# Splitting layer 1's mixer weights ahead, during layer 0's feed-forward, in a two-layer diffusion trunk on one core

## The chip, the core and the metric

The kernel runs on one NeuronCore of a Trainium2 chip. Its engines work side by side, each through its own queue of instructions in order: TensorE (PE, matrix products into PSUM), VectorE (DVE), ScalarE (ACT), GpSimd (POOL), and SyncE (SP), which here only issues transfers. GpSimd can issue transfers too. The metric is the device time of one execution in microseconds (us).

## The reference, cut to what matters

Two layers work on 512 latent tokens and 256 context tokens of width 1024, in float32. Layer 0 is attention beside a RWKV-7 recurrence, layer 1 a bidirectional RG-LRU block; each layer ends in a squared-ReLU feed-forward of width 4096.

```python
def trunk_layer(x, xc, c, c_ctx, mixer_fn, ...):
    mod_l = jnp.split(jax.nn.silu(c) @ mod_w + mod_b, N_MOD, axis=-1)
    ...
    y_l, y_c = mixer_fn(modulate(x, sh1, sc1), modulate(xc, csh1, csc1), *mixer_params, ctx_out=ctx_out)
    x = layer_norm(DEEPNORM_ALPHA * x + g1 * y_l, ln1_g, ln1_b)
    x = layer_norm(DEEPNORM_ALPHA * x + g2 * squared_relu_mlp(modulate(x, sh2, sc2), mlp_w1, mlp_w2), ln2_g, ln2_b)

def odd_mixer(hl, hc, w_in, conv_w, conv_b, ga_w, ga_b, gx_w, gx_b, lam, w_out, ctx_out):
    gate_l, xr_l = jnp.split(hl @ w_in, 2, axis=-1)
    ...
    xr_l = depthwise_conv(xr_l, conv_w, conv_b)
    ...
    y_lat = (jax.nn.gelu(gate_l) * (hs_l[0] + hs_l[1])) @ w_out
```

The matrix in question is layer 1's `w_in`, 1024 by 2048: columns 0 to 1023 make the gate, 1024 to 2047 the recurrence's input.

## The kernel before

**Products.** A float32 matrix is split in two parts that TensorE takes at its faster rate: `hi`, a copy rounded by a cast, and `lo`, the rest. A product is three matmuls per 128 rows of depth (`mm3`, lines 183 to 185): hi by hi, lo by hi, hi by lo. Weights come in tiles of 128 columns, `[128, 8, 128]`, 512 KB. `w_raw` (line 152) loads one on SyncE's queue into a buffer `wraw` (two of them), and `w_split` casts it to `whi` on ScalarE (line 130) and subtracts to `wlo` on VectorE (line 136); of `whi` and `wlo` there are three buffers each. A tile's buffers come free when its products are done. Products land in one of three PSUM banks `mm`, which come free when VectorE or ScalarE has read them.

**The feed-forward** (`mlp`) goes through the hidden width in four chunks. In each, eight tiles of the first matrix give products for two halves of the 768 tokens, 384 each; ScalarE takes the ReLU from PSUM (`mr`, line 425), VectorE squares it (`msq`, line 427), and the two split it to `uhi` and `ulo`. Then eight tiles of the second matrix give products that VectorE adds to `t` (line 450). In the last chunk the second matrix is gone through once for each half of the tokens, and each half is followed by its layer norm (`ln_half`): `lnrs` on GpSimd (line 347), `xn` on ScalarE, `hhi` and `t` on VectorE, some of `hlo` on GpSimd (line 396). The norm's output is the mixer's input.

**Fillers.** `fill`, called once per weight tile, runs the next entry of a list of side jobs. In layer 0's feed-forward these are 40 steps for the first sixteen blocks of layer 1's modulation. They load a tile of the modulation's weights into a buffer `mraw` (two of them), and `paced` queues each step's VectorE work behind the last product. When the first half's layer norm starts, all entries that are left run at once. Sixteen more modulation blocks (`mods_spare`, lines 247 to 257) follow the feed-forward: load to `mraw`, eight matmuls into `md`, a transpose.

**Layer 1's mixer** (`layer1_mixer`) goes through eight blocks of 128 channels. For each it takes one tile for the recurrence's input (`xt`) and one for the gate (`gt`) through `w_tiles`, evacuates (`xp`, line 576), convolves (`cy`, lines 589 and 591), casts and subtracts (`cyh`, `cyl`), makes four small products with the gate weights (`gwr`, line 581, split to `gwh`, `gwl`), takes tanh, exponential and square root (`ga`, `gx`, `tv`, line 624) and scans (line 643).

**Order.** A scheduler puts the instructions of each engine in order when the kernel is built, by its own times; the program's order decides where these are equal. `issue_after(x)` keeps an instruction behind x. Waits between engines are semaphores.

## Time and profile before

| | |
|---|---|
| median of 3 runs | 2084.34 us |
| these runs | 2079.3, 2084.34, 2087.86 us |
| profiled execution, own time | 2087.57 us |
| its span, first to last instruction | 2085.8 us |
| TensorE busy | 1932.2 us, 93% |
| VectorE busy | 1257.9 us, 60% |
| ScalarE busy | 852.5 us, 41% |
| GpSimd busy | 283.9 us, 14% |

Shares over the whole span are means over unlike stages. Times in the trace count from the span's start: layer 0's feed-forward lies from about 860 to 1436 us, its second layer norm ends near 1460, layer 1's mixer follows until about 1620. Chunk 2's second product lies from 1225 to 1293, chunk 3's first from 1293 to 1360, its second from 1360 to 1436.

### The profile page before, as it was taken

The page shows a single profiled execution, that of the slowest core. Times are in us where ns is not written, and L with a number is a line of the kernel's source. Part 1 is how long each engine was busy: PE and PEld are TensorE (multiplying, and loading weights), DVE is VectorE, ACT ScalarE, POOL GpSimd, SP SyncE. Part 2 cuts the span into 40 slices and gives each one's busy share as a digit, 9 for nine tenths or more (in the row PEclk, how much of TensorE's full clock was granted, in tenths as well). Part 3 has the DMA queues.
Part 4 walks back from the last instruction along what each step waited for, and adds up shares of the span by engine and source line. Part 5 has one row for each costly group of instructions (what it writes and reads, how often), then busy time and mean ns, then how long its engine had stood idle before and what let it go on. Part 6 is the DMA issues. An engine that isn't in the chain of part 4 may idle for free.

```text
span 2085.8 us, 39869 instructions
## 1 busy us (share of the span) xinstructions
PE 1932.2 (93%) x16130; PEld 1730.5 (83%) x16130; DVE 1257.9 (60%) x2583; ACT 852.5 (41%) x1479; POOL 283.9 (14%) x458
## 2 busy tenths in 40 slices
PE   7989888588999988999999999999989889999997
PEld 5767767466777767999999999998777779999997
DVE  4568766746666678774654333447699575444456
ACT  2555432524455443441231221334699444233242
POOL 0001222634435431100000000001000010000000
PEclk9999989889999998999999999999999999999999
DMA  9465544643423228332232222245521673333334
GB/s 348 140 190 179 146 132 117 171 115 93 125 65 91 67 67 253 101 87 84 83 103 81 61 61 61 66 126 157 151 72 56 199 196 102 98 96 94 99 102 142
DMA packets 411512, 249.21 MB, mean 119 GB/s; under 512 B 61200, under 2 KB 396096, under 8 KB 411200
## 3 DMA queue, kind: packets, MB, share of 16 engines
q1 hardware_dynamic: 408296, 243.58, 39.4%
q0 software_dynamic: 2848, 3.03, 0.7%
q8 instruction: 127, 2.08, 0.4%
q14 instruction: 57, 0.47, 0.1%
q10 hardware_dynamic: 184, 0.06, 0.0%
HBM read 209.38 MB, written 36.44 MB: 118 GB/s over the span
## 4 chain that ended last, share of the span: by engine, by line
PE 73%; DVE 10%; DMA 7%; ACT 5%; issue 2%; SPq 2%; POOL 0%; DVEq 0%; ACTq 0%; POOLq 0%
PE mm L183 18%; PE mm L184 18%; PE mm L185 18%; PE tr L183 2%; PE tr L184 1%; PE tr L185 1%; PE mm L883 1%; DVE wlo L136 1%; PE g L1393 1%; PE mm L874 1%; ACT whi L130 1%; DMA wraw<-in_l_mlp_w_dram 1%; DVE pr L1010 1%; PE g L1370 1%; DMA st<-rw_pq 1%
## 5 line engine op out<-in xcount | busy, mean ns | idle before, releaser
L183 PE MATMUL mm<-hhi,whi 128*128 128x384 f32 (+2 forms) x1504 | 491.8, 327 | 9.4 <-ACT f_k L719 6.1
L184 PE MATMUL mm<-hlo,whi 128*128 128x384 f32 (+2 forms) x1504 | 489.2, 325 | 0.6 <-DVE hlo L396 0.3
L185 PE MATMUL mm<-hhi,wlo 128*128 128x384 f32 (+2 forms) x1504 | 489.1, 325 | 0.0
L130 ACT CAST whi<-wraw 128x1024 fp32r<-128x1024 f32 x216 | 226.3, 1049 | 533.6 <-PE mm L184 444.8
L183 PE MATMUL mm<-uhi,whi 128*128 128x384 f32 (+1 forms) x1280 | 399.1, 312 | 4.6 <-DVE t L450 3.7
L185 PE MATMUL mm<-uhi,wlo 128*128 128x384 f32 (+1 forms) x1280 | 397.3, 311 | 3.6 <-DVE wlo L136 3.6
L184 PE MATMUL mm<-ulo,whi 128*128 128x384 f32 (+1 forms) x1280 | 396.7, 310 | 0.7 <-DVE ulo L136 0.7
L136 DVE TENSOR_TENSOR wlo<-wraw,whi 128x1024 fp32r<-128x1024 f32 x216 | 264.0, 1223 | 189.4 <-ACT whi L130 189.0
L183 PEld LDWEIGHTS mm<-hhi,whi 128*128 128x128 f32 x1504 | 287.8, 191 | 23.4 <-ACT f_k L719 6.3
L184 PEld LDWEIGHTS mm<-hlo,whi 128*128 128x128 f32 x1504 | 288.1, 192 | 11.6 <-DVE hlo L396 0.6
L185 PEld LDWEIGHTS mm<-hhi,wlo 128*128 128x128 f32 x1504 | 287.8, 191 | 11.4 <-issue 0.6
L183 PEld LDWEIGHTS mm<-uhi,whi 128*128 128x128 f32 x1280 | 243.0, 190 | 6.5 <-DVE t L450 4.0
L185 PEld LDWEIGHTS mm<-uhi,wlo 128*128 128x128 f32 x1280 | 243.1, 190 | 5.7 <-DVE wlo L136 4.9
L184 PEld LDWEIGHTS mm<-ulo,whi 128*128 128x128 f32 x1280 | 243.2, 190 | 1.3 <-DVE ulo L136 1.3
L450 DVE SCALAR_TENSOR_TENSOR t<-mm,g,t 128x256 f32<-128x256 f32 (+2 forms) x200 | 92.9, 481 | 226.9 <-PE mm L185 224.4
L347 POOL TENSOR_TENSOR lnrs<-lnrs,mhalf 128x1 f32<-128x1 f32 x20 | 10.7, 545 | 1007.6 <-DVE lnrs L346 1007.6
L1415 POOL TENSOR_SCALAR ds<-rv,rw_dd 64x64 f32<-64x64 f32 x176 | 85.7, 487 | 155.2 <-DVE rv L1429 144.6
L425 ACT ACTIVATE mr<-mm 128x384 f32<-128x384 f32 (+1 forms) x128 | 55.6, 434 | 83.5 <-PE mm L185 83.4
L130 ACT CAST uhi<-msq 128x384 fp32r<-128x384 f32 (+1 forms) x128 | 58.6, 458 | 75.8 <-DVE msq L427 75.8
L427 DVE SCALAR_TENSOR_TENSOR msq<-mm,mr 128x384 f32<-128x384 f32 (+1 forms) x128 | 62.3, 487 | 45.1 <-ACT mr L425 44.8
L136 DVE TENSOR_TENSOR ulo<-msq,uhi 128x384 fp32r<-128x384 f32 (+1 forms) x128 | 63.0, 492 | 33.2 <-ACT uhi L130 29.5
L1429 DVE SCALAR_TENSOR_TENSOR rv<-z,rw_dd,ds 64x64 f32<-64x64 f32 x176 | 49.7, 282 | 30.6 <-PE z L1427 25.8
(427 smaller groups left out, 2937.8 us busy)
## 6 DMA issues: line engine op xcount, KB each, us to landing
wraw<-in_l_mlp_w_dram SPq DMA_DIRECT2D x148, 512.0 KB
mraw<-in_l_mod_w_dram SPq DMA_DIRECT2D x48, 512.0 KB
wraw<-in_l_w_in_dram SPq DMA_DIRECT2D x36, 512.0 KB
wraw<-in_l_w_out_dram SPq DMA_DIRECT2D x32, 512.0 KB
mw<-in_l_mod_w_dram SPq DMA_DIRECT2D x16, 512.0 KB
wraw<-in_l_mod_w_dram SPq DMA_DIRECT2D x16, 512.0 KB
rw_pq<-pqbk SPq DMA_DIRECT2D x8, 768.0 KB
rw_bk<-pqbk SPq DMA_DIRECT2D x8, 768.0 KB
```

The costliest lines, as they stand in the source:

```text
L130: nc.scalar.copy(hi, src)
L136: e.tensor_tensor(out=lo, in0=src, in1=hi.bitcast(F32), op=ALU.subtract)
L183: nc.tensor.matmul(out, sh, mh, start=f, stop=False)
L184: nc.tensor.matmul(out, sh, ml, start=False, stop=False)
L185: ins = nc.tensor.matmul(out, sl, mh, start=False, stop=l)
L425: nc.scalar.activation(r, ps, AF.Relu)
L427: nc.vector.scalar_tensor_tensor(out=sq, in0=ps, scalar=0.0, in1=r, op0=ALU.max, op1=ALU.mult)
L450: nc.vector.scalar_tensor_tensor(out=t[:, m, x:y], in0=ps[:, x - a:y - a], scalar=g[:, m, s:s + 1], in1=t[:, m, x:y], op0=ALU.mult, op1=AL ...
L874: nc.tensor.transpose(ps[:, j * 128:(j + 1) * 128], p[:, (j0 + j) * 128:(j0 + j + 1) * 128], self.ident)
L883: nc.tensor.matmul(po[64 * e:64 * e + 64, :256], va[:, k0 // 128 + j, h * 64:(h + 1) * 64], pts[e][:, j, :], start=(j == 0), stop=(j == n ...
L1415: P.tensor_scalar(out=ds[d][H[e]], in0=rv[H[e], i, e, :], scalar1=dn[H[e]], scalar2=None, op0=ALU.mult)
L1429: V.scalar_tensor_tensor(out=rn[H[e], e, :], in0=zu[d][H[e], 1], scalar=dn[H[e]], in1=ds[d][H[e]], op0=ALU.mult, op1=ALU.add)
```

## The change

`presplit` makes a list of sixteen pieces, one for each 128 columns of `l1_w_in`. A piece loads its raw tile on GpSimd's queue into one `mraw` buffer, casts it on ScalarE into the other (`issue_after` the last `mr`), subtracts on VectorE in place (`issue_after` the last `msq`), and stores both to memory (`w_pre`) on GpSimd's queue. The pieces are appended to the fillers of layer 0's feed-forward, behind the 40 modulation steps, each followed by an empty entry. In the mixer `w_pre` loads the two split halves on SyncE's queue straight into `whi` and `wlo`; its casts and subtractions of `w_in`, and their `wraw` loads, are gone.

```diff
+    def presplit(self, ap, n):
+        nc = self.nc
+        self.pre = self.dram.tile([n, 2, 128, 8, 128], F32, name="w_pre")
+        for j in range(n):
+            raw, hi = (self.wp.tile([128, 8, 128], F32, tag="mraw", name=self.nm("mraw"), bufs=2) for _ in range(2))
+            lo = raw.bitcast(F32R)
+            nc.gpsimd.dma_start(raw, ap[:, 128 * j:128 * j + 128].rearrange("(k p) c -> p k c", p=128))
+            with self.tc.issue_after(self.paces[0].ins):
+                nc.scalar.copy(hi.bitcast(F32R), raw)
+            with self.tc.issue_after(self.paces[1].ins):
+                nc.vector.tensor_tensor(out=lo, in0=raw, in1=hi, op=ALU.subtract)
+            for i, x in enumerate((hi, raw)):
+                nc.gpsimd.dma_start(self.pre[j, i], x)
+            yield
+
+    def w_pre(self, js):
+        for i, j in enumerate(js):
+            w = [self.wp.tile([128, 8, 128], F32R, tag=t, name=self.nm(t), bufs=self.wbufs[1]) for t in ("whi", "wlo")]
+            for u, x in enumerate(w):
+                self.nc.sync.dma_start(x.bitcast(F32), self.pre[j, u])
+            yield i, w
...
-                    nc.scalar.activation(r, ps, AF.Relu)
+                    self.paces = [nc.scalar.activation(r, ps, AF.Relu)]
...
-                    nc.vector.scalar_tensor_tensor(out=sq, in0=ps, scalar=0.0, in1=r, op0=ALU.max, op1=ALU.mult)
+                    self.paces.append(nc.vector.scalar_tensor_tensor(out=sq, in0=ps, scalar=0.0, in1=r, op0=ALU.max, op1=ALU.mult))
...
-            xt, gt = self.w_tiles(w_in[:, D:2 * D], eng=XS), self.w_tiles(w_in[:, 0:D], eng=GS)
+            xt, gt = self.w_pre(range(8, 16)), self.w_pre(range(8))
...
                 self.fillers += [lambda b=b: run(self.mods_spare(1, [b])) for b in range(MODV, 16)]
+                ahead = self.presplit(I["l1_w_in"], 16)
+                self.fillers += [lambda: next(ahead), lambda: None] * 16
```

Three places of the built order. The first is VectorE at the start of chunk 2's second product; `t` is an evacuation (its product's number behind `mm`), `wlo` the split of a later tile. Before:

```order
L450 SCALAR_TENSOR_TENSOR t_9086<-mm_12885,g_0_9065,t_9086 128x384
L450 SCALAR_TENSOR_TENSOR t_9086<-mm_12911,g_0_9065,t_9086 128x128
L450 SCALAR_TENSOR_TENSOR t_9086<-mm_12911,g_0_9065,t_9086 128x256
L136 TENSOR_TENSOR wlo_13059<-wraw_13056,whi_13058 128x1024
L450 SCALAR_TENSOR_TENSOR t_9086<-mm_12944,g_0_9065,t_9086 128x384
```

Now:

```order
L475 SCALAR_TENSOR_TENSOR t_9086<-mm_12893,g_0_9065,t_9086 128x384
L475 SCALAR_TENSOR_TENSOR t_9086<-mm_12919,g_0_9065,t_9086 128x128
L475 SCALAR_TENSOR_TENSOR t_9086<-mm_12919,g_0_9065,t_9086 128x256
L136 TENSOR_TENSOR wlo_13081<-wraw_13078,whi_13080 128x1024
L186 TENSOR_TENSOR mraw_13071<-mraw_13071,mraw_13072 128x1024
L475 SCALAR_TENSOR_TENSOR t_9086<-mm_12959,g_0_9065,t_9086 128x384
L475 SCALAR_TENSOR_TENSOR t_9086<-mm_12985,g_0_9065,t_9086 128x128
L475 SCALAR_TENSOR_TENSOR t_9086<-mm_12985,g_0_9065,t_9086 128x256
L136 TENSOR_TENSOR wlo_13140<-wraw_13137,whi_13139 128x1024
L186 TENSOR_TENSOR mraw_13196<-mraw_13196,mraw_13197 128x1024
```

A piece's subtraction (`mraw`, line 186 now) stands between the split of a later tile and the next evacuation, here and for the two tiles that follow: four pieces in a row. Six more stand in the last product and its first layer norm.

The second place is GpSimd at the first half's layer norm. Before, its queue held only the norm's work there:

```order
L347 TENSOR_TENSOR lnrs_14174<-lnrs_14174,mhalf 128x1 [waits DVE_49,Pool_49]
L347 TENSOR_TENSOR lnrs_14195<-lnrs_14195,mhalf 128x1 [waits DVE_49,Pool_49]
L347 TENSOR_TENSOR lnrs_14216<-lnrs_14216,mhalf 128x1 [waits DVE_49,Pool_49]
L396 TENSOR_TENSOR hlo_9118<-hf_14235,hhi_9117 128x384 [waits DVE_49,PE_49]
```

Now (a wait on DMASW is one for a transfer of GpSimd's own queue):

```order
L188 DMA w_pre<-mraw_14206 128x1024 [waits DMASW6_49,DVE_49]
L182 DMA mraw_14245<-in_l_w_in_dram 128x8x128 [waits DMASW5_49,DMASW3_49]
L372 TENSOR_TENSOR lnrs_14287<-lnrs_14287,mhalf 128x1 [waits DVE_49,Pool_49]
L372 TENSOR_TENSOR lnrs_14308<-lnrs_14308,mhalf 128x1 [waits DVE_49,Pool_49]
L188 DMA w_pre<-mraw_14246 128x1024 [waits Activation_49]
L188 DMA w_pre<-mraw_14245 128x1024 [waits DMASW1_49,DVE_49]
L372 TENSOR_TENSOR lnrs_14329<-lnrs_14329,mhalf 128x1 [waits DVE_49,Pool_49]
L182 DMA mraw_14252<-in_l_w_in_dram 128x8x128 [waits DMASW6_49,DMASW0_49]
L421 TENSOR_TENSOR hlo_9118<-hf_14348,hhi_9117 128x384 [waits DVE_49,PE_49]
```

The loads and stores of pieces 13 and 14 stand among the norm's instructions, each load behind the landing of the store before it.

The third place is SyncE at the end of the feed-forward; `w_out` and `w_in` are the mixer's weights. Before:

```order
L152 DMA wraw_15030<-in_l_w_in_dram 128x8x128 [waits DMAHW7_49,DVE_49]
L152 DMA wraw_15089<-in_l_w_in_dram 128x8x128 [waits DMAHW0_49,DVE_49]
L1662 DMA t_spill<-t_9086 1024x1x384 [waits DMAHW3_49,DVE_49]
L152 DMA wraw_15148<-in_l_w_in_dram 128x8x128 [waits DMAHW1_49,DVE_49]
L152 DMA wraw_15181<-in_l_w_in_dram 128x8x128 [waits DMAHW5_49,DMAHW2_49,DVE_49]
L247 DMA mraw_14768<-in_l_mod_w_dram 128x8x128 [waits PE_49]
```

Now:

```order
L1688 DMA t_spill<-t_9086 1024x1x384 [waits DVE_49]
L272 DMA mraw_14813<-in_l_mod_w_dram 128x8x128 [waits DMASW4_49,DMASW2_49,DMASW6_49,DMASW0_49,Activation_49]
L152 DMA wraw_16782<-in_l_w_out_dram 128x8x128 [waits DMAHW4_49,DVE_49]
L196 DMA whi_15143<-w_pre 128x1024 [waits DMASW1_49,PE_49]
L196 DMA wlo_15144<-w_pre 128x1024 [waits PE_49]
L272 DMA mraw_14830<-in_l_mod_w_dram 128x8x128 [waits DMASW5_49,DMASW7_49,DMASW3_49,DMASW1_49]
```

Modulation block 16 (`mraw_14813`) and the first split tile of the mixer now stand behind a wait for GpSimd's transfers. On TensorE the eight matmuls of that block stand ahead of the last two transposes of `t` for the second half's norm.

## Rows read from the trace of the kernel before

**Rows 1.** Busy us of each engine by stage, with calls, granted clock, DMA share
```profile
core 0: us, PE busy (x) PEld busy (x) DVE busy (x) ACT busy (x) POOL busy (x), PEclk, DMA share, GB/s
1150.00:1300.00 150.00, 150.00 (x865) 149.03 (x864) 52.47 (x85) 34.45 (x53) 0.00 (x0) 1.00 0.22 64
1300.00:1400.00 100.00, 100.00 (x598) 99.31 (x596) 43.77 (x66) 32.49 (x49) 1.05 (x2) 1.00 0.30 90
1500.00:1620.00 120.00, 107.88 (x575) 93.82 (x574) 114.24 (x150) 111.02 (x137) 0.66 (x1) 0.94 0.25 71
```

**Rows 2.** Waits of TensorE, 1380 to 1660: total us, times, longest us
```profile
PE tr L183 <- DVE cyh L134: 5.6, 2, 5.4
PE tr L183 <- ACT ga L624: 4.0, 2, 3.2
```

**Rows 3.** Groups of VectorE and ScalarE, 1500 to 1620: busy us, mean ns
```profile
L136 DVE TENSOR_TENSOR wlo<-wraw,whi 128x1024 fp32r<-128x1024 f32 x10 | 12.2, 1216 | 0.0
L130 ACT CAST whi<-wraw 128x1024 fp32r<-128x1024 f32 x10 | 10.4, 1043 | 1.5 <-PE mm L184 1.5
```

**Rows 4.** TensorE in order of time from 1533: start, us, [idle before]
```profile
1533.79 1.19 PE L183 MATMUL tr<-cyh,gwh 128*128 128x512 f32 x2 [5.42 <-DVE cyh L134]
...
1537.22 0.63 PE L184 MATMUL tr<-cyl,gwh 128*128 128x512 f32 x1
1537.65 0.63 PE L185 MATMUL tr<-cyh,gwl 128*128 128x512 f32 x1
...
1540.56 0.28 PE L184 MATMUL tr<-cyl,gwh 128*128 128x256 f32 x1
```

**Rows 5.** Groups of VectorE and ScalarE in the feed-forward, 1150 to 1400
```profile
L136 DVE TENSOR_TENSOR wlo<-wraw,whi 128x1024 fp32r<-128x1024 f32 x34 | 41.7, 1225 | 49.2 <-ACT whi L130 49.2
...
L130 ACT CAST whi<-wraw 128x1024 fp32r<-128x1024 f32 x33 | 34.7, 1051 | 125.0 <-PE mm L184 125.0
...
L425 ACT ACTIVATE mr<-mm 128x384 f32<-128x384 f32 x32 | 15.6, 488 | 22.8 <-PE mm L185 22.8
```

**Rows 6.** Transfers by GpSimd's queue: count, KB each, median us from issue to landing
```profile
dx<-X POOLq DMA_DIRECT2D x8, 48.0 KB, 2.1
...
t<-dx POOLq DMA_DIRECT2D x16, 24.0 KB, 2.8
...
X<-dat POOLq DMA_DIRECT2D x12, 12.0 KB, 2.4
...
gbc<-in_l_ln_g_dram POOLq DMA_DIRECT2D x1, 512.0 KB, 4.7
bbc<-in_l_ln_b_dram POOLq DMA_DIRECT2D x1, 512.0 KB, 5.0
```

**Rows 7.** VectorE in order of time, chunk 2's second product
```profile
1267.75 0.74 DVE L450 SCALAR_TENSOR_TENSOR t<-mm,g,t 128x128 f32<-128x128 f32 x2 [3.62 <-PE mm L185]
...
1276.23 0.74 DVE L450 SCALAR_TENSOR_TENSOR t<-mm,g,t 128x128 f32<-128x128 f32 x2 [3.62 <-PE mm L185]
```

**Rows 8.** VectorE in order of time, chunk 3's second product and first norm
```profile
1389.10 0.62 DVE L450 SCALAR_TENSOR_TENSOR t<-mm,g,t 128x384 f32<-128x384 f32 x1 [2.06 <-PE mm L185]
...
1393.29 0.62 DVE L450 SCALAR_TENSOR_TENSOR t<-mm,g,t 128x384 f32<-128x384 f32 x1 [2.06 <-PE mm L185]
...
1423.19 1.21 DVE L136 TENSOR_TENSOR wlo<-wraw,whi 128x1024 fp32r<-128x1024 f32 x1
1424.32 0.35 DVE L392 CAST hhi<-hf 128x384 fp32r<-128x384 f32 x1
1424.59 0.67 DVE L394 TENSOR_SCALAR t<-tr,vcol 128x384 f32<-128x384 f32 x1
...
1435.94 0.74 DVE L450 SCALAR_TENSOR_TENSOR t<-mm,g,t 128x128 f32<-128x128 f32 x2 [2.38 <-PE mm L185]
```

**Rows 9.** The chain of waits that ended last, 1460 to 1470
```profile
1462.25 4.85 DMA mraw<-in_l_mod_w_dram
```

**Rows 10.** Waits of SyncE's queue, 1380 to 1660: total us, times, longest us
```profile
SPq L581 <- DVE gwl L136: 39.3, 6, 9.4
```

More of the change, by code (lines that the diff above doesn't have):

```diff
@@ L512 @@
 EARLY = {1: 1, 2: 1, 3: 1, 4: 1, 5: 1, 6: 1}
-XS, GS, OS = ("act", "dve"), ("act", "dve"), ("act", "dve")
+OS = ("act", "dve")
 GE, HS, GW = 2, 4, 1
@@ L555, in layer1_mixer @@
             spans = ((0, NL, 0), (NL, T, XO))
-            w_in = I["l1_w_in"]
             cw = self.cols["l1_conv_w"]
```

## The prediction

> **What bounds the kernel now.** Read the times by stage first [rows 1]. In the feed-forward of layer 0 (the stretches 1150 to 1300 and 1300 to 1400) TensorE is busy for all of its time at full clock, VectorE for 35 to 44% and ScalarE for 23 to 32%: TensorE sets the time there, and what VectorE and ScalarE are given costs nothing as long as TensorE does not wait for it. In layer 1's mixer, 1500 to 1620, it is the other way round: VectorE is busy for 114.2 of 120 us, ScalarE for 111.0, TensorE for 107.9 at a mean granted clock of 0.94. What TensorE waits for there [rows 2] is mostly the conv output's cast on VectorE (`cyh`) and ScalarE's tanh (`ga`), 9.6 us together. The weight splits stand among just that work: 10 subtractions, 12.2 us, and 10 casts, 10.4 us [rows 3].
>
> **What the change removes.** Sixteen casts (1.05 us) and sixteen subtractions (1.22 us) leave the mixer; ten of each lie in the crowded 120 us. VectorE falls there from 114.2 to 102.0 and ScalarE from 111.0 to 100.6, both below TensorE's 107.9, which then bounds. At most TensorE gets back its idle 12.1 us and what the slow clock took: after the wait for `cyh` (5.42 us) it ran at half clock, 1.2 GHz, from 1533.8 until 1540.6 [rows 4] (its 512-column products start 0.43 us apart there): half of those 6.7 us, 3.3, are the clock's. That makes 15. At least 4, if only the wait for `ga` goes, which stands behind ScalarE's casts. The chain tanh, exp, square root, scan stays, so I take **9**, which is the `cyh` wait with its slow clock.
>
> **What it adds: a chain.** Splitting ahead costs ScalarE 16 x 1.05 and VectorE 16 x 1.22 us in a stretch with room [rows 5], and 24 MB more traffic in a stretch whose DMA share is 0.2 to 0.3: nothing by themselves. What counts is that a piece (I number them 0 to 15) needs both `mraw` buffers, so the next piece's load waits until the low half of the last is stored. From one subtraction to the next there lies a cycle C: store, load, cast, subtraction. ScalarE and VectorE work in order, so whatever stands behind the cast and the subtraction waits for it.
>
> C by rows [rows 6]: the two 512 KB transfers from GpSimd's queue landed 4.7 and 5.0 us after issue. I take 4.85 for the store. The load has 1024 runs of 512 B against their 128 of 4 KB; from 192 runs (12 KB, 2.4 us) to 384 (24 KB, 2.8 us) landing grew by 2.1 ns a run, so 896 runs more cost 0 to 1.9 us; I take half, 5.7 us. With 1.05 + 1.22 that is **C = 12.8 us**; the near ends are 11.7 (4.7 twice) and 14.2 (6.9 and 5.0), the far one, if a transfer cost only the 2.1 us of the smallest store, 6.5.
>
> *Chunk 2's second product.* The order of VectorE shows pieces 2 to 5 one after another, each behind the evacuation of one weight tile's products and the split of another; they are not held to a fresh product, because `paces` still names the last one of the first matrix. A weight tile takes 8.48 us there and half of it 4.24 [rows 7]; C is longer. Let T be the end of the last first-matrix product. Piece 1 is subtracted at T + 2.8 (evacuation 0.49 [rows 5], cast, subtraction), piece 5 at T + 2.8 + 4C = T + 54.0. Behind it on VectorE is the evacuation of the fifth tile, and TensorE has three `mm` banks: the second half of the sixth tile, its twelfth half, needs one of the banks that this evacuation frees. It would start at T + 11 x 4.24 = T + 46.6; it starts at T + 54.6. **8.0 us** (3.6 at C = 11.7, 13.6 at 14.2, none below 10.8). ScalarE's casts for later tiles come in time, since three weight buffers put them two tiles ahead. After the wait the clock is low once more: **3.3**, as after `cyh`.
>
> *Chunk 3's last product and the layer norm.* Pieces 6 to 9 are four products apart (17 us) and cost nothing. Pieces 9 to 15 follow each other through a stage that is 4.19 us a tile [rows 8], ending with the layer norm of the first half, because the eight fillers that are left are run at its start. Let U be the end of the last first-matrix product, eight tiles of 4.19 ahead of 1393.3, so 1359.8. Piece 9 is subtracted at U + 2.8, piece 15 at U + 2.8 + 6C = U + 79.6. Behind it stand `hhi` (0.35), `t` (0.67) and the split of the very last tile (1.21): that is ready at U + 81.8. TensorE started that tile at 1435.94 - 4.19, U + 71.9. **9.8 us** (3.2 and 18.2 at the near ends, none below 11.2). GpSimd's queue has the norm's `lnrs` and three `hlo` behind these waiting transfers too; their lateness lies inside the same cycles, and I add nothing for it.
>
> *Behind that.* On SyncE the next modulation load (`mraw`, block 16) waits for piece 15's low half to land, and the first reloaded mixer weights stand behind it. On TensorE that block's products stand ahead of the transposes of the layer norm's second half. The block is ready at piece 15 + 4.85 (store) + 4.85 (the load that TensorE is seen to wait for [rows 9]) = + 9.7; TensorE has finished the last tile at + 2.2 + 4.19 = + 6.4. **3.3 us**.
>
> **Sum**: 8.0 + 3.3 + 9.8 + 3.3 - 9 = +15.4 against the profiled execution's 2087.6, so 2103.0; that execution is 3.2 above the median of the three, so the forecast is **2100 us**. With C = 11.7 it is +4.4 (+9.4 with the smallest gain, -1.6 with the largest), with 14.2 +29.4, or +34 with the smallest gain.
>
> **Rivals.** *The chain is short enough.* Place: the same pieces. If store and load together take less than 8.5 us (C below 10.8), both waits vanish, the block-16 load is early, and only the mixer's gain is left: 2084 - 9 = **2075**, 2069 to 2080. For it: small transfers on that queue landed in 2.1 us, and nothing in this trace stores 512 KB from GpSimd's queue to memory. Against: both 512 KB rows. The Trainium skill, "DMA: Bandwidth & Descriptors", section on the anatomy of a SWDGE DMA, gives about 2.0 us + bytes/436e3 for one such transfer: 3.2 us for 512 KB, an estimate from that page, so C = 8.7 and this rival's time. Where the trace has that size it disagrees: 4.7 and 5.0 us, and the measurement decides.
>
> *The reloads come late in the mixer.* Each weight tile now needs two 512 KB loads into buffers that come free only when the tile three before is used up, so there is less lead than with a raw tile in between. Between release and need lie two products and a block, some 14 us; the loads need 4.85 and about 2 more. But SyncE's queue is in order and waited for the gate weights' split up to 9.4 us at a time [rows 10]: 9.4 + 6.9 is 2.3 beyond the lead, and six such waits are 14 us on top of the sum: **2114**. Against: with less on VectorE that split comes earlier.
>
> Also against the change speaks the Trainium skill, "SBUF — State Buffer", section "SBUF: two separate sides": GpSimd cannot write descriptors while VectorE runs an fp32 copy in its two-port mode. VectorE does such a copy (`hhi`, eight a half) just where pieces 13 to 15 run; no run here shows what it costs, it would lengthen C, and nothing is added for it.
>
> **Chances.** Forecast 0.56, short chain 0.32, late reloads 0.12. A measurement of this kernel can tell about 0.5%, 10.4 us, from no change. Half of the short-chain case gains more than that: faster 0.16. Its other half and the part of the forecast with C near 12 or a large mixer gain are the same: 0.16 + 0.16. The rest is slower: 0.52. As the cases have both signs, the range reaches from the middle of the short-chain case to the late reloads: **2072 to 2120**; the forecast's own is 2083 to 2118.
>
> **What would show it.** Right: TensorE waits of 2 to 5 us in chunk 2's second product (around 1265 to 1285), released by `t` on VectorE, where it had none; VectorE's waits ended by ScalarE's cast of `mraw`, and ScalarE's by the load; pieces 12 to 13 us apart; the mixer shorter by 5 to 12 us, with VectorE's share down and TensorE's near full. Wrong: pieces 8.5 us apart in that product and TensorE still at 100% there; or a mixer that is no shorter, with TensorE waiting for DMA of `whi` or `wlo`.

## The result, and the profile after

The changed kernel takes 2101.15 us in the median of 12 runs, the kernel before 2082.43 in 12 runs beside it: a ratio of 1.0075, 95% interval 1.0058 to 1.0092. It is slower by about 16 us by that ratio (the medians lie 18.7 apart); 2100 was forecast. The profiled execution took 2103.06 us, with a span of 2101.3, 15.5 longer than the span of before. The total is right; most of the terms that make it up are not, and this section shows where each came out.

For the whole of the document the span is cut at marks that VectorE's rows give: the first square (`msq`) of layer 0's feed-forward, the last one of chunk 0, the last one of chunk 3, the last addition to `t` in that feed-forward, the first and the eighth of the mixer's sums (`hs`), the first square of layer 1's feed-forward, the end. What lies ahead of the first mark varied from 871 to 884 us between executions and has nothing of the change in it, so it is left out of the sums. One execution of each kernel was traced, and the last stage ("rest"), whose program text is the same in all, came out between 371 and 376 us: a difference of 2 or 3 us in one stage of one trace is not clear of noise by itself.

| us from mark to mark | before | changed |
|---|---|---|
| squares of chunk 0 | 70.8 | 71.9 |
| to the last square of chunk 3 | 407.3 | 408.4 |
| last product and first half's norm | 74.1 | 85.5 |
| to the mixer's first sum | 77.2 | 83.7 |
| first to eighth sum | 122.4 | 120.0 |
| to layer 1's feed-forward | 76.5 | 76.6 |
| rest | 373.8 | 373.8 |
| sum | 1202.2 | 1220.0 |

Two rows hold the loss: +11.4 in the last product with the first norm, +6.5 from there to the mixer's first sum. The mixer gives back 2.4.

Busy times by stretch, the same ones as in [rows 1], with the two stretches of the norms between them (busy us and calls for each engine, then granted clock, DMA share, GB/s):

```profile
core 0: us, PE busy (x) PEld busy (x) DVE busy (x) ACT busy (x) POOL busy (x), PEclk, DMA share, GB/s
1150.00:1300.00 150.00, 149.13 (x860) 147.83 (x859) 58.22 (x90) 40.34 (x59) 11.99 (x18) 1.00 0.40 127
1300.00:1400.00 100.00, 93.94 (x544) 93.67 (x542) 45.43 (x60) 36.76 (x53) 11.96 (x18) 0.99 0.57 174
1400.00:1436.00 36.00, 31.28 (x179) 30.58 (x180) 28.13 (x52) 17.52 (x20) 11.37 (x16) 0.90 0.70 214
1436.00:1460.00 24.00, 20.79 (x139) 18.85 (x137) 9.79 (x27) 2.83 (x4) 1.63 (x3) 0.93 1.00 325
1500.00:1620.00 120.00, 114.64 (x685) 100.63 (x684) 98.05 (x144) 100.66 (x131) 0.00 (x0) 0.99 0.44 141
```

Up to 1300 TensorE loses 0.9 us; from 1300 to 1436, 10.8. What it waited for, from 1150 to 1480 (total us, times, longest):

```profile
PE tr L355 <- DVE lnst L358: 9.1, 3, 7.8
PE tr L409 <- ACT xn L382: 3.2, 2, 2.1
PE mm L208 <- DMA whi<-w_pre: 1.8, 1, 1.8
PE md L276 <- DMA mraw<-in_l_mod_w_dram: 1.7, 1, 1.7
PE mm L208 <- DVE t L475: 0.9, 1, 0.9
```

**The chain in chunk 2.** VectorE in order of time (start, us, what, idle before it and its releaser):

```profile
1238.02 1.23 DVE L186 TENSOR_TENSOR mraw<-mraw,mraw 128x1024 fp32r<-128x1024 f32 x1 [3.13 <-ACT mraw L184]
...
1248.12 1.23 DVE L186 TENSOR_TENSOR mraw<-mraw,mraw 128x1024 fp32r<-128x1024 f32 x1 [4.75 <-ACT mraw L184]
...
1258.84 1.23 DVE L186 TENSOR_TENSOR mraw<-mraw,mraw 128x1024 fp32r<-128x1024 f32 x1 [6.99 <-ACT mraw L184]
...
1269.94 1.23 DVE L186 TENSOR_TENSOR mraw<-mraw,mraw 128x1024 fp32r<-128x1024 f32 x1 [7.57 <-ACT mraw L184]
1271.08 1.26 DVE L475 SCALAR_TENSOR_TENSOR t<-mm,g,t 128x384 f32<-128x384 f32 x3
```

The pieces do stand in VectorE's way, each later than the last, since they come 10.1 to 11.2 us apart and a weight tile takes 8.48. The evacuations behind the last three come three at a time. TensorE's banks just last: it waits 0.9 us for `t`, and the clock stays at 1.00. The cycle, by ScalarE (first and last row) and GpSimd's queue:

```profile
1236.94 1.05 ACT L184 CAST mraw<-mraw 128x1024 fp32r<-128x1024 f32 x1 [3.31 <-DMA mraw<-in_l_w_in_dram]
...
1238.28 0.55 POOL L188 DMA_DIRECT2D w_pre<-mraw  x1 [5.25 <-ACT mraw L184]
...
1241.78 0.91 POOL L182 DMA_DIRECT2D mraw<-in_l_w_in_dram  x1 [1.70 <-DMA w_pre<-mraw]
...
1247.04 1.05 ACT L184 CAST mraw<-mraw 128x1024 fp32r<-128x1024 f32 x1 [4.93 <-DMA mraw<-in_l_w_in_dram]
```

From the cast's start to the issue of the high half's store are 1.3 us, from there to the next load's issue 3.5, from there to the next cast 5.3: 10.1. The load waits for the store of the high half; the prediction had it wait for that of the low half. Between pieces 11 and 12 it is plain (the two issues, and the low half's time from issue to landing):

```profile
1389.69 0.53 POOL L188 DMA_DIRECT2D w_pre<-mraw  x1 [0.71 <-DVE mraw L186]
1391.93 0.91 POOL L182 DMA_DIRECT2D mraw<-in_l_w_in_dram  x1 [1.71 <-DMA w_pre<-mraw]
...
w_pre<-mraw POOLq DMA_DIRECT2D x1, 512.0 KB, 5.5
```

The load is issued 2.2 us after the low half's store, 3.3 before that has landed. All 15 loads behind a piece are issued 0.3 to 1.5 us after its high half has landed, 14 of them before its low half has. So the next raw tile takes the buffer of the high half, and the subtraction and the low half's store run beside the cycle, not in it.

**The chain at the norm.** VectorE, and then TensorE, behind the last first-half product:

```profile
1393.11 0.62 DVE L475 SCALAR_TENSOR_TENSOR t<-mm,g,t 128x384 f32<-128x384 f32 x1 [0.40 <-PE mm L210]
1399.90 1.23 DVE L186 TENSOR_TENSOR mraw<-mraw,mraw 128x1024 fp32r<-128x1024 f32 x1 [6.18 <-ACT mraw L184]
1401.05 1.29 DVE L358 BATCH_NORM_STATS2 lnst<-tr 128x6 f32<-128x512 f32 x2
```

```profile
1392.91 1.04 PE L355 MATMUL tr<-ident,t 128*128 128x128 f32 x8
1401.79 1.97 PE L355 MATMUL tr<-ident,t 128*128 128x128 f32 x8 [7.85 <-DVE lnst L358]
...
1403.88 0.52 PE L209 MATMUL mm<-ulo,whi 128*128 128x384 f32 x1
1404.20 0.52 PE L210 MATMUL mm<-uhi,wlo 128*128 128x384 f32 x1
```

The transposes for the first half's statistics are in their bank by 1393.9. The statistics (`lnst`) stand behind piece 12's subtraction, which waits for its cast, which waits for the load: 6.2 us of idle VectorE. TensorE can't transpose the next tokens until the bank is read. It waits 7.85 us and then runs at half clock, 1.2 GHz: its 384-column products start 0.32 us apart until 1407.4, where they started 0.174 apart before. From 1393.1 to the next addition to `t` are 16.6 us; before, from 1393.29 [rows 8] to this row, they were 6.8:

```profile
1400.08 0.74 DVE L450 SCALAR_TENSOR_TENSOR t<-mm,g,t 128x128 f32<-128x128 f32 x2 [0.85 <-PE mm L185]
```

**Behind it.** SyncE's queue at the end of the feed-forward:

```profile
1437.26 0.59 SPq L1688 DMA_DIRECT2D t_spill<-t  x1
1438.02 0.80 SPq L272 DMA_DIRECT2D mraw<-in_l_mod_w_dram  x1
1438.92 2.90 SPq L152 DMA_DIRECT2D wraw<-in_l_w_out_dram  x1
1441.92 3.14 SPq L196 DMA_DIRECT2D whi<-w_pre  x1
```

`t_spill` starts once VectorE is past piece 15's subtraction, the load of block 16 (`mraw`) once that piece's high half has landed (1437.7), and the rest behind it; from 1436 to 1460 the DMA share is 1.00 at 325 GB/s. TensorE's waits for `whi` and `wlo` (1.8 and 0.5 us) lie here, that for `mraw` (1.7) just behind, and ScalarE is busy for 2.8 of those 24 us.

**The mixer.** TensorE's waits from 1500 to 1660, to be held against [rows 2]:

```profile
PE tr L208 <- ACT ga L648: 5.7, 5, 3.9
PE tr L208 <- DVE cyh L134: 2.4, 1, 2.4
```

From 1500 to 1620 VectorE is at 98.1 us and ScalarE at 100.7 (forecast: 102.0 and 100.6), but that stretch begins 31 us ahead of the first sum here and 13 ahead of it before. From the first to the eighth sum, before and changed:

```profile
1513.10:1635.50 122.40, 109.13 (x584) 93.81 (x582) 114.37 (x150) 107.94 (x131) 1.09 (x2) 0.94 0.24 69
1530.80:1650.80 120.00, 110.34 (x637) 95.30 (x635) 106.40 (x149) 100.85 (x125) 1.03 (x2) 0.96 0.37 119
```

VectorE has lost 8.0 us and ScalarE 7.1; the wait for `cyh` has halved, that for `ga` has grown by 1.7; and the eight sums come only 2.4 us sooner after one another.

### The profile page after: what moved, and what is told of

Its sections match the earlier page's. It is cut to its first block, busy times and chain, and to the rows that moved or that the text cites. A ratio compares the mean times of both kernels' runs of the same rounds, so it can differ in the third digit from the quotient of the medians.

```text
span 2101.3 us, 39995 instructions
## 1 busy us (share of the span) xinstructions
PE 1937.8 (92%) x16130; PEld 1735.0 (83%) x16130; DVE 1257.6 (60%) x2583; ACT 852.9 (41%) x1479; POOL 316.3 (15%) x506
## 4 chain that ended last, share of the span: by engine, by line
PE 65%; DMA 10%; DVE 8%; issue 8%; ACT 5%; POOL 2%; SPq 1%; DVEq 0%; ACTq 0%; POOLq 0%
PE mm L208 15%; PE mm L209 15%; PE mm L210 15%; DMA w_pre<-mraw 2%; PE tr L208 2%; DMA wraw<-in_l_w_out_dram 2%; PE tr L210 2%; PE tr L209 2%; DVE wlo L136 1%; PE mm L907 1%; PE g L1417 1%; PE mm L898 1%; ACT whi L130 1%; DMA wraw<-in_l_mlp_w_dram 1%; PE g L1394 1%
## 5 line engine op out<-in xcount | busy, mean ns | idle before, releaser
L130 ACT CAST whi<-wraw 128x1024 fp32r<-128x1024 f32 x200 | 209.6, 1050 | 485.7 <-PE mm L209 378.4
L136 DVE TENSOR_TENSOR wlo<-wraw,whi 128x1024 fp32r<-128x1024 f32 x200 | 245.4, 1228 | 187.7 <-ACT whi L130 187.3
L475 DVE SCALAR_TENSOR_TENSOR t<-mm,g,t 128x256 f32<-128x256 f32 (+2 forms) x200 | 92.4, 480 | 193.0 <-PE mm L210 190.4
L372 POOL TENSOR_TENSOR lnrs<-lnrs,mhalf 128x1 f32<-128x1 f32 x20 | 10.8, 548 | 509.2 <-DVE lnrs L371 509.2
```

The source lines that it names most:

```text
L130: nc.scalar.copy(hi, src)
L136: e.tensor_tensor(out=lo, in0=src, in1=hi.bitcast(F32), op=ALU.subtract)
L475: nc.vector.scalar_tensor_tensor(out=t[:, m, x:y], in0=ps[:, x - a:y - a], scalar=g[:, m, s:s + 1], in1=t[:, m, x:y], op0=ALU.mult, op1=AL ...
```

## The experiments

Ratios are to the kernel before, on the same chip; stage times are from the profiled execution, cut at the marks above. The edits are shown against the changed kernel where nothing else is said.

**The two sides apart.** First the mixer alone, with one piece split:

```diff
-                self.nc.sync.dma_start(x.bitcast(F32), self.pre[j, u])
+                self.nc.sync.dma_start(x.bitcast(F32), self.pre[j % 1, u])
-                self.fillers += [lambda: next(ahead), lambda: None] * 16
+                self.fillers += [lambda: next(ahead), lambda: None] * 1
```

> The mixer's side alone: one piece instead of sixteen is split in the feed-forward, and all sixteen mixer tiles are loaded from that one pair, same size and runs as in the changed kernel (so the mixer multiplies with the wrong weights for fifteen tiles). Theory A, TensorE's own floor: in the changed kernel's trace the mixer, from the end of the second norm to the last of its eight sums, is 3 us shorter than before although VectorE has 14 us less to do, because TensorE is busy 158 of 171 us; then this kernel is 3 to 4 us faster than before (2079, ratio 0.998) with the feed-forward as before. Theory B, the gain was 9 us as forecast and the late start of the reloads took 6 of it: 9 us faster (2073, ratio 0.9957).

Measured: 1.0004 (0.9988 to 1.0020). Neither. The sums lie 120.2 us apart, as in the changed kernel, so the late start took nothing from the mixer's gain (B falls); but 78.3 us pass from the last addition to the first sum, 1.1 more than before, and the timed gain that A expected is not there (this trace's stages sum to 1199.1, 3.1 less than before; the twelve timed runs do not bear that out). The mixer's side of the change is worth next to nothing by itself.

Then the pieces alone:

```diff
-            xt, gt = self.w_pre(range(8, 16)), self.w_pre(range(8))
+            xt, gt = self.w_tiles(I["l1_w_in"][:, D:2 * D]), self.w_tiles(I["l1_w_in"][:, 0:D])
```

> The feed-forward's side alone: all sixteen pieces are split and stored as in the changed kernel, but the mixer loads and splits the raw weights as the kernel before does. Theory A: the pieces cost 11 us up to the last product of the feed-forward (piece 12 ahead of the first norm's statistics on VectorE) and 7 us more up to the end of the second half's norm, both by themselves; with no gain in the mixer this is 18 us slower than before (2100, ratio 1.0087). Theory B: the 7 us come from the reloads of split weights, which share a full DMA with the modulation's and the output weights' loads just there; then it is 11 us slower (2093, ratio 1.005).

Measured: 1.0108 (1.0088 to 1.0129). The last product with the first norm takes 83.4 us (+9.3) and the stretch to the first sum 82.1 (+4.9): both by the pieces themselves, as A has it, though 4 us less than A's 18. The same place is named, 5.2 us for the statistics:

```profile
PE tr L355 <- DVE lnst L358: 6.0, 2, 5.2
```

The rest is in the mixer, whose sums lie 127.3 us apart here, 4.9 more than before with the same program text. Which order or transfer does that, no run tells.

**Without the last four pieces.**

```diff
-                self.fillers += [lambda: next(ahead), lambda: None] * 16
+                self.fillers += [lambda: next(ahead), lambda: None] * 12
-                self.nc.sync.dma_start(x.bitcast(F32), self.pre[j, u])
+                self.nc.sync.dma_start(x.bitcast(F32), self.pre[j % 12, u])
```

> Only pieces 0 to 11; the last four are left out, and the mixer's tiles 12 to 15 load pieces 0 to 3 instead (wrong weights in four tiles). Theory A: piece 11 is off VectorE by about 1389.5, ahead of the first norm's statistics at 1393.5, so TensorE's waits for them (9.1 us and the slow clock behind) vanish, and the block of the modulation that stood behind piece 15 comes in time too: about 18 us faster than the changed kernel, 3 us faster than before (2079, ratio 0.9985). Theory B, reloads: the first wait goes (11 us), the 7 us in the second half's norm stay: 4 us slower than before (2086, ratio 1.002).

Measured: 1.0013 (0.9999 to 1.0027). Both losses of the changed kernel go: 75.5 us for the last product and norm (85.5 there), 77.9 to the first sum (83.7), 17.0 us less in the sum of stages (1203.0). The wait for the statistics is down to

```profile
PE tr L355 <- DVE lnst L358: 1.0, 2, 0.6
```

That is A's mechanism. But the time is that of the kernel before, not 3 us under it: once more the mixer's side brings next to nothing.

**Spread out.** All sixteen pieces, among the modulation steps instead of behind them:

```diff
-                self.fillers += [lambda: self.paced(spare)] * (MODV // 2 * 5)
-                self.fillers += [lambda: next(ahead), lambda: None] * 16
+                m, p = lambda: self.paced(spare), lambda: next(ahead)
+                self.fillers += [m, m, p, m, m, m, p] * 8
```

> All sixteen pieces, spread over the feed-forward: one after the second and one after the fifth of each block pair's five modulation steps, so all are done before chunk 3's second product; nothing is left out. Theory A: pieces 25 to 34 us apart hide a chain of 12 us wholly; no TensorE wait in the feed-forward or the norm is new, and what is left is the mixer's 3 us: 3 to 4 us faster than before (2079, ratio 0.998). Theory B: modulation steps and pieces now wait for each other's two buffers, the next modulation load waits on SyncE's queue for a piece's stores with the feed-forward's weight loads behind it, and TensorE waits in chunks 0 to 3 for raw weights: over 5 us slower than before (2088 or more).

Measured: **0.9936** (0.9921 to 0.9952), 2066.5 us: faster than both kernels, and by four times what A expected. The last subtraction is at 1333.3, ahead of chunk 3's second product; the last product and norm take 74.5 us, and TensorE is busy for all but 0.4 us from 1300 to 1436:

```profile
1300.00:1400.00 100.00, 99.65 (x607) 97.80 (x606) 50.51 (x92) 33.88 (x50) 3.60 (x6) 1.00 0.45 137
1400.00:1436.00 36.00, 36.00 (x234) 35.33 (x233) 24.09 (x54) 10.70 (x15) 4.54 (x6) 1.00 0.60 199
```

Its stages are 13.3 us shorter than before. Chunk 0 takes 67.5 us (3.3 less), but chunks 1 to 3 take 410.4 (3.1 more): 13 of TensorE's matmuls have moved out of chunk 0, and up to the last square both kernels take 478 us for 2762 matmuls. The gain lies behind: 7.8 us in the stretch to the first sum (69.4), 2.4 among the eight sums (120.0), and 3 behind the eighth sum, where the text is that of before. From the last addition to the eighth sum, before and spread:

```profile
1435.90:1635.50 199.60, 180.19 (x1121) 154.07 (x1118) 162.48 (x249) 156.38 (x209) 5.92 (x14) 0.95 0.36 102
1432.30:1621.70 189.40, 176.97 (x1120) 151.99 (x1118) 145.76 (x235) 143.88 (x195) 5.85 (x14) 0.97 0.46 149
```

For as many matmuls TensorE is idle for 12.4 us, not 19.4, and busy for 3.2 us less at a higher mean clock. Of the waits in [rows 2] that for `cyh` is gone; its longest now are

```profile
PE tr L208 <- ACT ga L648: 5.8, 5, 3.9
PE tr L209 <- DVE cyl L136: 1.5, 2, 1.4
```

No sum had this gain ahead of the first sum, so two more kernels asked for it: the kernel before with only its modulation steps spread, and other places for the pieces.

```diff
-                self.fillers += [lambda: self.paced(spare)] * (MODV // 2 * 5)
+                m, p = lambda: self.paced(spare), lambda: None
+                self.fillers += [m, m, p, m, m, m, p] * 8
```

> The kernel before, with nothing split ahead, but with its 40 modulation steps spread as in the spread kernel (an empty entry where that one has a piece). In the spread kernel's trace the 13 us are: 3 in chunk 0, 8 from the last product of the feed-forward to the first of the mixer's eight sums, 2 among the eight sums. Theory A, splitting ahead pays the last two: only chunk 0's 3 us appear here (2078, ratio 0.9985). Theory B, the gain is the modulation's new places, splitting ahead pays nothing by itself: about 13 us faster than before here too (2068, ratio 0.994).

Measured: 0.9973 (0.9954 to 0.9993). Between the two, nearer to A: chunk 0 takes 66.8 us, and the wait of 2.0 us for `msq` that TensorE had in chunk 0 before is gone, with fewer modulation steps in that stretch on VectorE; up to the last square of chunk 3 it takes 475.9 us, 2.2 less than before. (The 3 us in chunk 0 that the expectation counts for the spread kernel are no gain there, as said above.) The stretch to the first sum is 75.3 (1.9 less), the sums 122.3, as before; TensorE's wait for `cyh` is down to 0.2 us here too, but another has come:

```profile
PE md L251 <- DVE modred L256: 6.5, 3, 5.3
```

So of the spread kernel's 0.64% some 0.27 come with the modulation's new places alone, and 0.37 (about 8 us; 0.1 to 0.6 by the two intervals) with the splitting ahead on top of them.

```diff
-                self.fillers += [m, m, p, m, m, m, p] * 8
+                self.fillers += [m, m, m, p, m, m, p] * 8
```

> The spread kernel with its pieces at other places: after the third and the fifth of each five modulation steps instead of after the second and the fifth. Theory A, what counts is that every piece is long done before chunk 3's second product: 2064 to 2071 (ratio 0.992 to 0.995). Theory B, the gain hangs on the exact order that was built: half of it or less (2074 or more).

(The diff is against the spread kernel.) Measured: 0.9936 (0.9913 to 0.9958). A: the gain does not hang on one order. It isn't spread over the stages in the same way, though: 73.2 us to the first sum here, 69.4 there. From the last addition to the eighth sum, with 1120 or 1121 matmuls in each, it is 199.6 us before, 197.6 with the modulation spread alone, 198.5 with the mixer's side alone (one piece), 189.4 and 193.0 with both: neither gives more than 2 us there by itself, the two together 10 and 7. Why they need each other is not settled. In the built orders 144 of TensorE's `w_in` matmuls stand ahead of the first gate product in all of these kernels; between the last addition and that product stand 72 modulation matmuls in the three spread ones, 80 before and in the changed kernel, 88 in the two without gain (one piece, twelve pieces). That alone is not it, since the kernel with the modulation spread alone has the 72 as well.

**Two pairs of buffers.**

```diff
-            raw, hi = (self.wp.tile([128, 8, 128], F32, tag="mraw", name=self.nm("mraw"), bufs=2) for _ in range(2))
+            raw = self.wp.tile([128, 8, 128], F32, tag="mraw", name=self.nm("mraw"), bufs=2)
+            hi = self.mt.tile([128, 8, 128], F32, tag="mhi", name=self.nm("mhi"), bufs=2)
```

> The changed kernel with one edit: a piece's high half goes to a buffer of its own (two of them, from a pool of the feed-forward), so two pieces can be under way at once. Theory A, the cycle is store, load, cast, subtraction through one pair of buffers: with two pairs the load of the next piece overlaps the store of the last, pieces in the second products come 8.5 us apart or closer, TensorE's 7.8 us wait for the first norm's statistics goes and the block behind it comes in time: 15 us or more faster than the changed kernel (2085 or less, ratio to before at most 1.001). Theory B, the transfers themselves are the limit (GpSimd's queue, or the issue of 0.9 and 2 x 0.5 us a piece, in a row with its waits): pieces stay 10 to 12 us apart and the time stays at 2096 to 2104.

Measured: 1.0029 (1.0008 to 1.0049). Between: pieces come in pairs 14 to 17 us apart, and the last is off VectorE at 1407, not 1436; the stretch to the first sum is 77.8 us again. But the last product with the norm still takes 82.7. Loads and stores overlap there now, and the DMA share from 1358 to 1392 is 0.96:

```profile
1358.00:1392.40 34.40, 32.51 (x190) 32.23 (x188) 18.80 (x22) 11.90 (x13) 8.51 (x13) 1.00 0.96 290
1392.40:1412.00 19.60, 15.38 (x86) 14.04 (x87) 11.95 (x25) 8.65 (x9) 5.30 (x9) 0.83 0.91 296
```

ScalarE's casts of the feed-forward's own weights wait for their loads (10.4 us in three waits, the longest 6.0), the subtractions and evacuations behind them come late, and TensorE waits 3.6 us for the statistics and 2.1 for `xn`, with a slow clock behind. Without the buffer wait the transfers fill the DMA engines, and the weight loads are late instead. (The traced execution took 2095.2 us, 7.5 more than the median of the ten.)

**Traffic without the work.** On the kernel with the pieces alone:

```diff
-            with self.tc.issue_after(self.paces[0].ins):
-                nc.scalar.copy(hi.bitcast(F32R), raw)
-            with self.tc.issue_after(self.paces[1].ins):
-                nc.vector.tensor_tensor(out=lo, in0=raw, in1=hi, op=ALU.subtract)
-            for i, x in enumerate((hi, raw)):
+            for i, x in enumerate((raw, raw)):
```

> The kernel with the pieces alone (mixer from raw weights), less their casts and subtractions: each of the sixteen pieces is loaded by GpSimd's queue and stored twice, raw, so the 24 MB of traffic stays and nothing of a piece stands on ScalarE or VectorE. Theory A, the pieces cost time by standing in the order of VectorE and ScalarE: no TensorE wait in the feed-forward is new, time as before (ratio 0.998 to 1.002). Theory B, they cost it by traffic, since in the changed kernel the DMA share rose from 0.41 to 0.78 in chunk 3's second product and ScalarE's casts waited up to 6 us for raw weights there: the feed-forward stays 5 us or more longer than before (ratio 1.003 to 1.008).

Measured: 0.9998 (0.9975 to 1.0020). A, with a limit: with nothing to wait for, the transfers run ahead and are over by 1237, in the stretch where a weight tile lasts 8.4 us. TensorE does not notice a DMA share of 0.92 there:

```profile
1150.00:1220.00 70.00, 70.00 (x407) 69.48 (x406) 27.46 (x47) 23.81 (x41) 19.89 (x30) 1.00 0.92 288
```

It says nothing on chunk 3's second product, where a tile lasts 4.19 us and the weights come twice as fast; there the two-buffer kernel shows late loads, and so does the changed kernel: from 1360 to 1400 ScalarE waits 6.3 us for raw weights, in two waits, and not at all before. What the traffic by itself costs there is not tested.

**What sets the mixer's pace.** Three cuts on the spread kernel, each by its profiled execution alone; what is read is the distance from the first to the eighth sum, 120.0 us there. TensorE's products:

```diff
             nc.tensor.matmul(out, sh, mh, start=f, stop=False)
+            if few and i < n - 1:
+                continue
             nc.tensor.matmul(out, sh, ml, start=False, stop=False)
```

(`few=True` is given for the mixer's `w_in` products alone.)

> The spread kernel with the mixer's w_in products cut from 24 matmuls to 10 each (the two lower-order matmuls are left out for seven of eight rows of depth); all loads, evacuations and the rest of the mixer stay. Eight sums lie 120 us apart from first to last in the spread kernel. Theory A, TensorE is the floor once the splits are gone: 14 matmuls fewer for each of 384, 384 and 512 columns are 8 us a block, so the sums lie near 70 to 90 us apart. Theory B, the chain of ScalarE and VectorE through one block (tanh, exponential, square root, scan) is the floor: still 105 us or more, with TensorE idle in between.

Measured: 120.9 us. From the first to the eighth sum, spread kernel and cut one:

```profile
1501.70:1621.70 120.00, 111.11 (x624) 96.76 (x622) 107.60 (x147) 103.00 (x128) 1.01 (x2) 0.97 0.35 114
1507.80:1628.70 120.90, 78.23 (x370) 64.16 (x371) 101.39 (x136) 97.07 (x115) 0.60 (x1) 0.76 0.27 87
```

TensorE is busy for 33 us less and the sums come no sooner. The mean granted clock fell from 0.97 to 0.76 with it, the small gate products in the chain were slower (605 ns against 448 in the mean for 512 columns of `cyh` by `gwh`), and its stages sum to 1206.1 us, 17.2 more than with all products. A falls: all the gate products together took 13.5 us more than in the spread kernel, so even with those taken off (an estimate from the two traces) the sums would lie 107 us apart, not 70 to 90.

```diff
-                act(tv, tv, AF.Sqrt, scale=0.25)
-                prev[0] = prev[1]
```

> The spread kernel without the mixer's square root (its eight activations of 1.49 us and their table loads on ScalarE are left out). With TensorE's w_in products cut by 14 of 24 the eight sums still lay 121 us apart, so TensorE is not the mixer's floor. Theory A, ScalarE's row of steps is (105 of 120 us busy): its 12 us and some 10 us of table loads come off, sums 95 to 105 us apart. Theory B, VectorE (108 of 120 us busy) is: sums still 113 us or more apart.

```diff
-                    for j in range(1, 4):
+                    for j in range(1, 2):
```

> The spread kernel with two of the three tap additions of the mixer's convolution left out on VectorE (32 of 48 instructions, 0.6 us each, 18 us). Theory A, ScalarE is the mixer's floor: sums 113 us or more apart. Theory B, VectorE is: sums about 102 to 108 us apart.

Measured: without the square root 112.0 us, 8.0 less; without the two taps 121.2, none less. VectorE is not the floor, which is what A expects of the second run. Of the first, 8 us came where A expected 15 to 25 and B 7 or less. The rows from the first to the eighth sum of the two:

```profile
1490.90:1602.90 112.00, 105.94 (x603) 92.07 (x603) 105.70 (x146) 82.48 (x111) 1.15 (x2) 1.00 0.35 118
1497.20:1618.40 121.20, 112.07 (x624) 98.02 (x622) 96.08 (x124) 102.73 (x128) 1.11 (x2) 0.96 0.34 113
```

Of 20.5 us taken from ScalarE 8 show; of 11.5 taken from VectorE, nothing. The kernel with cut products has no engine that is busy for more than 102 of its 120.9 us, so the pace there is not any engine's sum but that of steps which follow one another through a block. ScalarE's are among them, the taps on VectorE are not. Why no more than 8 came is open: without the square root TensorE is busy for 105.9 of the 112.0 us at full clock and VectorE for 105.7, so those two leave little more to gain.

## Why the prediction was right, and where it was not

The forecast of +15.4 on the profiled execution met +15.5 on the span, of which 2.3 are a shorter front; on the stages after it, it is +17.8. That is three terms too small and one too large, and that they met within 0.1 us is luck: the term for chunk 2 is 10 us too high, the mixer's gain 6.6 too high, the two others 1.6 and 3.2 too low. Of the signs that the prediction named, the waits of VectorE for the cast and of ScalarE for the load are there; TensorE's waits of 2 to 5 us in chunk 2 (0.9), pieces 12 to 13 us apart there (10.1 to 11.2) and a mixer 5 to 12 us shorter (2.4) are not.

- **Chunk 2's second product: 8.0 + 3.3 forecast, about 1 measured.** The chain is there: VectorE waiting for ScalarE's cast of `mraw`, ScalarE for the load, the pieces further apart than the tiles. But its cycle is not the one that I priced. I let the next load wait for the low half's store, which put the subtraction (1.22 us) into the cycle; it waits for the high half's, which is issued right behind the cast. And for the store I took 4.85 us, from loads; the next load was issued 3.5 us after the high half's store. With 1.3 for the cast and the issue behind it and 5.3 for the load (I took 5.7), C was 10.1 in the cycle shown and at most 11.2, not 12.8. The text had the threshold, "none below C = 10.8", and the mean of the four cycles is 10.8. The profile gives medians of 3.8 us for the 32 stores and 5.1 for the loads, from issue to landing:

```profile
w_pre<-mraw POOLq DMA_DIRECT2D x32, 512.0 KB, 3.8
...
mraw<-in_l_w_in_dram POOLq DMA_DIRECT2D x16, 512.0 KB, 5.1
```

  The Trainium skill, "DMA: Bandwidth & Descriptors", section on the anatomy of a SWDGE DMA, gives 3.2 us for this size (2.0 us + bytes/436e3, an estimate from that page). That is near the stores where the DMA engines had room (3.0 us in the median from 1230 to 1290) and 2 us below the loads.
- **The last product with the first norm: 9.8 forecast, 11.4 measured, at another place.** I looked for the wait behind piece 15, at the very last tile. It came behind piece 12, at the norm's first statistics. The prediction's own numbers held it: piece 12 is due at U + 2.8 + 3C = U + 41.2 (it came at U + 40.1), the statistics could have been read from U + 34 on, and the order that stands ahead of the prediction shows GpSimd's share of that place. Once TensorE had been held up there, the later pieces cost little more: from 1409.7 on the stage is 1.6 us longer than before. A chain that is late is paid for once, at the first place where something stands behind it. C was 12.2 on the average here, where the DMA share was 0.78 (1361.6 to 1400) and 0.70 (1400 to 1436) and the loads of pieces 10 to 12 landed 6.7 us after issue in the median. That is near the 12.8, but by slower loads and not by the terms that I added up.
- **Block 16 and the queue behind it: 3.3 forecast, 6.5 measured.** The order was read rightly but for the half: SyncE issued block 16's load at 1438.02, behind the landing of piece 15's high half (1437.7; the low half, which I named, landed at 1439.7), and the first split tile behind that. Yet TensorE did not wait for block 16. Its matmuls run at 1447.24, right behind the last tile, which was late itself. The waits came behind that, for `whi` and `wlo` (1.8 and 0.5), a later block (1.7) and `xn` (1.0), with a mean granted clock of 0.92 up to the first sum where it was 0.96. What I left out is that all the transfers held up there then start together (a DMA share of 1.00). With the mixer as before the pieces cost 4.9 of the 6.5, with a clock of 0.90.
- **The mixer: -9 forecast, -2.4 measured.** This is the step that was wrong in kind. I let both busy sums fall below TensorE's and concluded that TensorE "then bounds", so that its idle time would come back. The cuts on the spread kernel speak against a bound by any one engine's sum. VectorE lost 8.0 us between the sums and ScalarE 7.1, and waits took much of their place: those of VectorE for `tv` rose from 10.5 to 16.6 us over the eight blocks, and ScalarE waits 11.7 us for products to evacuate where it had no such wait. So the splits had largely filled gaps in the chain. What I forecast, TensorE's wait for `cyh` with its slow clock given back, did come in the spread kernel (10.2 us from the last addition to the eighth sum, 7.0 of them idle time), where the modulation's steps had moved too; why it needs both is open.

The rival of the short chain was right on the second product of chunk 2 and wrong on the norm, and its 9 us from the mixer were not there either. The late reloads did not happen: in the mixer TensorE does not wait for a transfer of `whi` or `wlo` after 1460. GpSimd's issues at the norm took 0.95 us for a load and up to 0.59 for a store, against 0.91 and 0.53 to 0.55 elsewhere, so the rule on `hhi` and GpSimd's descriptors that the prediction names from the Trainium skill, "SBUF — State Buffer", section "SBUF: two separate sides", shows nothing here that would be worth a term.

## What to carry to other kernels

A side job with a transfer cycle in it cost no TensorE time here while its pieces came further apart than the cycle and the DMA engines had room (a share of 0.45 in the spread kernel); let it end before the stretch where the tiles get short or a norm begins. The same sixteen pieces were 16 us of loss at the end of the feed-forward and, spread over it with the modulation's steps, part of a gain of 13. When a cycle is priced, find in the built order which store a load waits for: here it was the first of two, and a step that I counted ran beside the cycle. And before work is taken off two full engines, see whether it stands in the chain or in its gaps: a cut of one step that is in the chain, beside a cut of one that is not, says more than their busy shares. Compare stages from mark to mark, not at equal times.

## What the runs showed of the hardware

With TensorE busy for 33 us less in 120, the kernel with cut products was 17 us longer than the one with all of them, in one execution of each. The mean granted clock (1.00 is 2.4 GHz, 0.50 is 1.2 GHz) stood at 0.85 in the stretch to the first sum, 0.76 among the sums and 0.89 behind them, against 0.98, 0.97 and 0.95; the stretches took 76.0, 120.9 and 80.6 us, against 69.4, 120.0 and 75.2. A part of the first difference may be the order, which was built anew with the shorter products (88 modulation matmuls ahead of the first gate product, 72 with all products); the runs don't separate the two. In these two executions, work that kept TensorE busy was not worth cutting for its own time.
